# A residual-add RMSNorm whose engines get programs, semaphores and a hardware loop of their own

## The chip, the cores and the metric

The kernel runs on one core of one Trainium2 chip. The metric is device time in microseconds (us), the median of several executions. A profile holds one execution, so a single profile differs from the median by a microsecond or two.

Engines in the profile: DVE is the vector engine, ACT the scalar engine, POOL is GpSimd, SP issues the DMA transfers, and "SPq" is SP's queue. 16 DMA engines move the data; a transfer is dealt out to all of them in packets: chained by their times, the packet records of the kernel before give each engine 1710 to 1714 of the 27392 packets of 57344 bytes, and 16 packets are under way at once for 98% of the time (100 to 3600 us). Tiles are counted from 0, as in the code.

## The reference

```python
batch, seq, dim = 32, 2048, 2048          # all float32
z = x + residual
rms = np.sqrt(np.mean(z ** 2, axis=-1, keepdims=True) + eps)
return (z / rms * gamma).astype(np.float32)
```

Two arrays of 537 MB are read and one is written: 1610.6 MB in all. There is little arithmetic to each byte.

## The kernel before

The 65536 rows are cut into 74 tiles of 128 partitions: 3 rows per partition in the first, 5 in the second, 7 in the other 72. Two slots `z` hold x and are overwritten with the sum and then the result; the residual goes to an area of 11 rows in which two tiles overlap. A tile framework orders the instructions, places the semaphores and writes the loop over tiles out in full.

```python
    def load_r(i):
        a = entry(i)
        nc.sync.dma_start(out=r_area[:, a : a + sizes[i], :], in_=rows(r_f, i))

    def add(i, a, b):
        z = z_slots[i % 2][:, a:b, :]
        o = entry(i)
        nc.vector.tensor_add(out=z, in0=z, in1=r_area[:, o + a : o + b, :])
    # ... square(): ACT, one row at a time, then the root; scale(): DVE ...

    def compute(i):
        # ... (last tile: four parts, interleaved) ...
        done = []
        for a, b in parts(i):                 # two parts
            add(i, a, b)
            done.append((a, b, square(i, a, b)))
        for d in done:
            scale(i, *d)

    # ... first loads, gamma ...
    compute(0)
    for i in range(1, n_tiles):
        store(i - 1)
        compute(i)
        if i + 1 < n_tiles:
            load_r(i + 1)                     # may start when the first add of tile i is through
            load_x(i + 1)                     # may start when store(i - 1) has landed
    store(last)
```

All three large transfers of a tile (7.3 MB each) go through SP's one queue, in the order store, residual, x.

## Time and profile before

The median was 3726.57 us (3726.44 to 3728.58, three runs).

| What | Value | Where it stands |
|---|---|---|
| span of the profiled run | 3724.8 us | head of the page |
| busy: data queue, DVE, ACT | 99.9%, 62%, 29% | queue table; busy table |
| rate in nearly every slice | 434 GB/s | the slices |
| one tile (three transfers of 7.3 MB) | 50.76 us | store to store in SP's timeline |
| instruction fetches | 20 packets of 8 KB | queue table, q14 |

The page of the kernel before: the head, the rate in 40 slices of the span, the DMA queues (packets, MB, share of the 16 engines' time) and the chain that ended last.

```profile
span 3724.8 us, 2571 instructions
DVE 2302.8 (62%) x816; ACT 1072.3 (29%) x1176; POOL 0.2 (0%) x4
GB/s 419 432 434 434 434 434 434 435 434 434 434 434 434 434 434 434 434 434 434 434 432 434 434 434 434 433 434 434 434 434 434 434 434 434 433 434 434 434 435 397
q1 hardware_dynamic: 32832, 1610.63, 99.9%
q14 instruction: 20, 0.16, 0.0%
DMA 67%; DVE 24%; ACT 8%; issue 0%; SPq 0%; DVEq 0%
```

The data queue is busy for 99.9% of the span and moves 434 GB/s in nearly every slice. The chain gives a third of the span to DVE and ACT, but it follows one slot around, and about half of the transfers' time in it is standing in the queue (34.6 us from a store's issue to its landing, 16.9 us of it moving data). An engine share in a chain is therefore not yet a limit.

SP's issues in the timeline of the kernel before (start us, duration us, queue, line, operation, what it moves):

```profile
1994.57 0.34 SPq L92 DMA_DIRECT2D out_dram<-z  x1
2018.89 0.33 SPq L84 DMA_DIRECT2D r_area<-in_residual_dram  x1
2029.14 0.33 SPq L88 DMA_DIRECT2D z<-in_x_dram  x1
2045.33 0.34 SPq L92 DMA_DIRECT2D out_dram<-z  x1
...
2096.09 0.34 SPq L92 DMA_DIRECT2D out_dram<-z  x1
...
2147.41 0.34 SPq L92 DMA_DIRECT2D out_dram<-z  x1
...
2198.17 0.34 SPq L92 DMA_DIRECT2D out_dram<-z  x1
```

From store to store a tile takes 50.76 us (2045.33 less 1994.57, and so on), which is 22.0 MB at 434 GB/s. One step is 51.32 us, from 2096.09 to 2147.41. The residual load is issued at 2018.89, the x load at 2029.14, when the store before has landed.

### The profile page before, as it was taken

The page shows a single profiled execution, that of the slowest core. Times are in us where ns is not written, and L with a number is a line of the kernel's source. Part 1 is how long each engine was busy: PE and PEld are TensorE (multiplying, and loading weights), DVE is VectorE, ACT ScalarE, POOL GpSimd, SP SyncE. Part 2 cuts the span into 40 slices and gives each one's busy share as a digit, 9 for nine tenths or more (in the row PEclk, how much of TensorE's full clock was granted, in tenths as well). Part 3 has the DMA queues.
Part 4 walks back from the last instruction along what each step waited for, and adds up shares of the span by engine and source line. Part 5 has one row for each costly group of instructions (what it writes and reads, how often), then busy time and mean ns, then how long its engine had stood idle before and what let it go on. Part 6 is the DMA issues. An engine that isn't in the chain of part 4 may idle for free.

```text
span 3724.8 us, 2571 instructions
## 1 busy us (share of the span) xinstructions
DVE 2302.8 (62%) x816; ACT 1072.3 (29%) x1176; POOL 0.2 (0%) x4
## 2 busy tenths in 40 slices
DVE  5666665566665566665566665566665566655566
ACT  2333322233322233322233322233322233322233
POOL 0000000000000000000000000000000000000000
DMA  9999999999999999999999999999999999999999
GB/s 419 432 434 434 434 434 434 435 434 434 434 434 434 434 434 434 434 434 434 434 432 434 434 434 434 433 434 434 434 434 434 434 434 434 433 434 434 434 435 397
DMA packets 32860, 1610.82 MB, mean 432 GB/s; under 512 B 3652, under 2 KB 3652, under 8 KB 3652
## 3 DMA queue, kind: packets, MB, share of 16 engines
q1 hardware_dynamic: 32832, 1610.63, 99.9%
q14 instruction: 20, 0.16, 0.0%
q10 hardware_dynamic: 8, 0.03, 0.0%
HBM read 1073.77 MB, written 536.87 MB: 432 GB/s over the span
## 4 chain that ended last, share of the span: by engine, by line
DMA 67%; DVE 24%; ACT 8%; issue 0%; SPq 0%; DVEq 0%
DMA z<-in_x_dram 34%; DMA out_dram<-z 33%; DVE z L97 15%; DVE z L125 9%; ACT sq_junk L103 8%; ACT rms L110 0%; DVE rstd L122 0%; SPq L84 0%; DVEq L97 0%; SPq L88 0%; DVE rstd_tail L122 0%; DVEq L122 0%
## 5 line engine op out<-in xcount | busy, mean ns | idle before, releaser
L97 DVE TENSOR_TENSOR z<-z,r_area 128x8192 f32<-128x8192 f32 (+2 forms) x150 | 1109.4, 7437 | 1272.7 <-DMA z<-in_x_dram 1270.5
L103 ACT ACTIVATE sq_junk<-z 128x2048 f32<-128x2048 f32 x512 | 963.4, 1882 | 2614.7 <-DVE z L97 2603.3
L125 DVE SCALAR_TENSOR_TENSOR z<-z,rstd,gamma_tile 128x2048 f32<-128x2048 f32 x505 | 1153.5, 2344 | 5.2
L122 DVE RECIPROCAL rstd<-rms 128x4 f32<-128x4 f32 (+2 forms) x146 | 25.3, 173 | 117.1 <-ACT rms L110 117.1
L103 ACT ACTIVATION_READ_ACCUMULATOR sq_junk<-z 128x1 f32 x512 | 95.4, 186 | 0.0
L110 ACT ACTIVATE rms<-ssq,eps_tile 128x4 f32<-128x4 f32 (+2 forms) x150 | 44.5, 297 | 4.8
L125 DVE SCALAR_TENSOR_TENSOR z<-z,rstd_tail,gamma_tile 128x2048 f32<-128x2048 f32 x7 | 16.2, 2344 | 0.1
L161 DVE LOAD_MASK_SELECT gamma_tile<-r_area x1 | 0.0, 14 | 11.4 <-DMA r_area<-in_gamma_dram 11.4
L103 ACT ACT_TABLE_LOAD x1 | 1.3, 1283 | 11.1 <-DMA z<-in_x_dram 11.1
L161 DVE STREAM_SHUFFLE gamma_tile<-r_area 128x2048 f32<-128x2048 f32 x1 | 2.3, 2294 | 0.0
L156 DVE MEMSET r_area<- 128x2048 f32 x1 | 1.8, 1765 | 0.4 <-issue 0.4
L110 ACT ACT_TABLE_LOAD x1 | 1.3, 1283 | 0.0
L122 DVE RECIPROCAL rstd_tail<-rms 128x2 f32<-128x2 f32 (+1 forms) x4 | 0.6, 162 | 0.2
L67 DVE MEMSET eps_tile<- 128x1 f32 x1 | 0.1, 59 | 0.8 <-PEq L192 0.8
L192 POOL MEMSET const-bfloat16-1.0<- 128x1 bf16 x1 | 0.1, 101 | 0.0
L192 POOL MEMSET const-uint8-127<- 128x1 uint8 x1 | 0.1, 101 | 0.0
L192 POOL MEMSET const-float32-0.0<- 128x1 f32 x1 | 0.1, 98 | 0.2 <-issue 0.2
L192 POOL MEMSET const-float32-1.0<- 128x1 f32 x1 | 0.1, 98 | 0.0
## 6 DMA issues: line engine op xcount, KB each, us to landing
r_area<-in_residual_dram SPq DMA_DIRECT2D x72, 7168.0 KB, 27.2
z<-in_x_dram SPq DMA_DIRECT2D x71, 7168.0 KB, 33.8
out_dram<-z SPq DMA_DIRECT2D x71, 7168.0 KB, 34.6
z<-in_x_dram SPq DMA_DIRECT2D x3, 2048.0 KB, 24.1
out_dram<-z SPq DMA_DIRECT2D x3, 2048.0 KB, 16.7
r_area<-in_residual_dram SPq DMA_DIRECT2D x1, 5120.0 KB, 29.4
z<-in_x_dram SPq DMA_DIRECT2D x1, 5120.0 KB, 42.5
out_dram<-z SPq DMA_DIRECT2D x1, 5120.0 KB
```

Of the source, the lines that this page charges most:

```text
L67: nc.vector.memset(eps_tile, float(eps))
L97: nc.vector.tensor_add(out=z, in0=z, in1=r_area[:, o + a : o + b, :])
L103: nc.scalar.activation(out=sq_junk, in_=z_slots[i % 2][:, a + g, :], func=Act.Square, accum_out=ssq[:, g : g + 1],)
L110: nc.scalar.activation(out=rms[:, :n], in_=ssq[:, :n], func=Act.Sqrt, bias=eps_tile, scale=inv_d)
L122: nc.vector.reciprocal(out=rstd[:, :n], in_=rms[:, :n])
L125: nc.vector.scalar_tensor_tensor(out=row, in0=row, scalar=rstd[:, g : g + 1], in1=gamma_tile, op0=mult, op1=mult,)
L156: nc.vector.memset(stage, 0.0)
L161: nc.vector.stream_shuffle(gamma_tile, stage, [0] * 32)
L192: nc = _bacc.Bacc("TRN2", target_bir_lowering=False, num_devices=1)
```

## The change

The intent is to take the ordering out of the framework's hands: each engine gets its own program, waits on semaphores named by the kernel, and runs tiles 3 to 70 in a hardware loop of its own, two tiles per iteration (34 iterations). Transfers, their sizes and order, and the vector and scalar instructions stay. The core of the diff, cut:

```diff
-    slots = ctx.enter_context(tc.tile_pool(name="slots", bufs=1))
+    z = [sb(f"z{p}", [P, R, D]) for p in range(2)]
+    names = ["x_in", "r_in", "s_out", "add_a", "add_b", "rms_a", "rms_b", "done"]
+    ev = {k: [sem(f"{k}{p}") for p in range(2)] for k in names}
+    def sp_turn(sp, t):
+        i = t.i
+        t.wait(sp, "done", -1)
+        inc(sp.dma_start(out=t.dram(o_f, o_full, -1), in_=z[(i - 1) % 2][...]), "s_out", i - 1)
+        ...
+        t.wait(sp, "add_a")
+        load_r(sp, t, 1)
+        t.wait(sp, "s_out", -1)
+        ...
+        load_x(sp, t, 1)
+    def dve_turn(v, t, own):
+        t.wait(v, "x_in")
+        t.wait(v, "r_in")
+        (a0, b0), (a1, b1) = parts(i)
+        inc(add(v, i, a0, b0), "add_a", i)
+        inc(add(v, i, a1, b1), "add_b", i)
+        for h, (a, b) in enumerate(parts(i)):
+            t.wait(v, "rms_a" if h == 0 else "rms_b")
+            ...                               # reciprocal, scale
+        inc(ins, "done", i)
+    @block.sync
+    def _(sp):
+        ...                                   # first loads, tiles 1 and 2
+        with sp.Fori(0, 2 * n_iter, 2) as it:
+            for i in range(LO, LO + 2):
+                sp_turn(sp, Turn(i, it))      # wait values and addresses from a register
+        ...                                   # last tiles, written out
+    @block.vector                             # and @block.scalar: the same shape
+    ...
+    nc.gpsimd.sem_clear(range(ids[0], ids[-1] + 1))
-    for i in range(1, n_tiles):
-        store(i - 1)
-        compute(i)
-        ...
```

More of the change, by code (lines that the diff above doesn't have):

```diff
@@ L38 @@
     STEP = 4
-    n_full = n_rows // (P * R)
-    left = (n_rows - n_full * P * R) // P
-    assert n_full * P * R + left * P == n_rows
+    U = 16
     lead = [3, 5]
-    assert left + R == sum(lead)
-    sizes = lead + [R] * (n_full - 1)
+    n_full = (n_rows // P - sum(lead)) // R
+    sizes = lead + [R] * n_full
     starts = [0]
@@ L47 @@
         starts.append(starts[-1] + P * k)
+    assert starts[-1] == n_rows
     n_tiles = len(sizes)
     last = n_tiles - 1
-    assert n_tiles >= 5
+    LO = 3
+    n_iter = (last - 1 - LO) // 2
+    HI = LO + 2 * n_iter
+    assert n_iter >= 1
     def rows(t, i):
@@ L54, in rows, with full, sb, ps @@
         return t[starts[i] : starts[i] + P * k, :].rearrange("(p r) m -> p r m", r=k)
+    def full(t):
+        return t[starts[2] :, :].rearrange("(n p r) m -> n p r m", p=P, r=R)
+    x_full, r_full, o_full = full(x_f), full(r_f), full(o_f)
     inv_d = 1.0 / float(D)
-    slots = ctx.enter_context(tc.tile_pool(name="slots", bufs=1))
-    stats = ctx.enter_context(tc.tile_pool(name="stats", bufs=6))
-    psum = ctx.enter_context(tc.tile_pool(name="psum", bufs=1, space=bass.MemoryType.PSUM))
-    z_slots = [slots.tile([P, R, D], fp32, name=f"z{k}") for k in range(2)]
-    r_area = slots.tile([P, R + STEP, D], fp32, name="r_area")
-    eps_tile = slots.tile([P, 1], fp32, name="eps_tile")
-    sq_junk = psum.tile([P, D], fp32, name="sq_junk")
-    gamma_tile = psum.tile([P, D], fp32, name="gamma_tile")
-    nc.vector.memset(eps_tile, float(eps))
+    def sb(name, shape):
+        return ctx.enter_context(nc.sbuf_tensor(name, shape, fp32))
+    def ps(name, shape):
+        return ctx.enter_context(nc.psum_tensor(name, shape, fp32))
+    sems = []
+    def sem(name):
+        sems.append(ctx.enter_context(nc.semaphore(name)))
+        return sems[-1]
+    ctx.enter_context(tc.tile_critical())
+    z = [sb(f"z{p}", [P, R, D]) for p in range(2)]
+    r_area = sb("r_area", [P, R + STEP, D])
+    eps_tile = sb("eps_tile", [P, 1])
+    ssq = [[sb(f"ssq{p}{h}", [P, 4]) for h in range(2)] for p in range(2)]
+    rms = [[sb(f"rms{p}{h}", [P, 4]) for h in range(2)] for p in range(2)]
+    rstd = [[sb(f"rstd{p}{h}", [P, 4]) for h in range(2)] for p in range(2)]
+    tail_ssq = sb("tail_ssq", [P, R])
+    tail_rms = sb("tail_rms", [P, R])
+    tail_rstd = sb("tail_rstd", [P, R])
+    sq_junk = ps("sq_junk", [P, D])
+    gamma_tile = ps("gamma_tile", [P, D])
+    names = ["x_in", "r_in", "s_out", "add_a", "add_b", "rms_a", "rms_b", "done"]
+    ev = {k: [sem(f"{k}{p}") for p in range(2)] for k in names}
+    x_tail = [sem(f"x_tail{k}") for k in range(4)]
+    g_in = sem("g_in")
+    dve = sem("dve_own")
+    act = sem("act_own")
+    s_tail = sem("s_tail")
+    tail_ev = {k: sem(f"tail_{k}") for k in ("add", "rms", "done")}
+    tail = [(0, 2), (2, 4), (4, 6), (6, 7)]
     def entry(i):
@@ L72, in entry @@
         return 0 if i % 2 else STEP
-    tail = [(0, 2), (2, 4), (4, 6), (6, 7)]
     def parts(i):
@@ L79, in parts @@
             return [(0, 2), (2, sizes[0])]
-        return [(STEP, sizes[i]), (0, STEP)] if i % 2 else [(0, R - STEP), (R - STEP, R)]
-    def load_r(i):
-        a = entry(i)
-        nc.sync.dma_start(out=r_area[:, a : a + sizes[i], :], in_=rows(r_f, i))
-    def load_x(i):
-        for a, b in tail if i == last else [(0, sizes[i])]:
-            nc.sync.dma_start(out=z_slots[i % 2][:, a:b, :], in_=rows(x_f, i)[:, a:b, :])
-    def store(i):
-        for a, b in tail if i == last else [(0, sizes[i])]:
-            nc.sync.dma_start(out=rows(o_f, i)[:, a:b, :], in_=z_slots[i % 2][:, a:b, :])
@@ L94, in add @@
-    def add(i, a, b):
-        z = z_slots[i % 2][:, a:b, :]
-        o = entry(i)
-        nc.vector.tensor_add(out=z, in0=z, in1=r_area[:, o + a : o + b, :])
-    def square(i, a, b):
-        n = b - a
-        ssq = stats.tile([P, 4], fp32, name="ssq")
-        for g in range(n):
-            nc.scalar.activation(
-                out=sq_junk,
-                in_=z_slots[i % 2][:, a + g, :],
-                func=Act.Square,
-                accum_out=ssq[:, g : g + 1],
-            )
-        rms = stats.tile([P, 4], fp32, name="rms")
-        nc.scalar.activation(
-            out=rms[:, :n], in_=ssq[:, :n], func=Act.Sqrt, bias=eps_tile, scale=inv_d
-        )
-        return rms
@@ L115, in scale @@
-    def scale(i, a, b, rms):
-        n = b - a
-        if i == last:
-            rstd = stats.tile([P, 4], fp32, name="rstd_tail", bufs=1)
-        else:
-            rstd = stats.tile([P, 4], fp32, name="rstd")
-        nc.vector.reciprocal(out=rstd[:, :n], in_=rms[:, :n])
-        for g in range(n):
-            row = z_slots[i % 2][:, a + g, :]
-            nc.vector.scalar_tensor_tensor(
-                out=row,
-                in0=row,
-                scalar=rstd[:, g : g + 1],
-                in1=gamma_tile,
+        k = sizes[i] if i < 2 else R
@@ new lines, in parts, with __init__, at, wait @@
+        return [(STEP, k), (0, STEP)] if i % 2 else [(0, R - STEP), (R - STEP, R)]
+    class Turn:
+        def __init__(self, i, it=None):
+            self.i, self.it, self.p = i, it, i % 2
+        def at(self, d):
+            n = ((self.i + d) // 2 + 1) * U
+            return n if self.it is None else self.it * (U // 2) + n
+        def wait(self, eng, kind, d=0):
+            eng.wait_ge(ev[kind][(self.i + d) % 2], self.at(d))
+        def dram(self, t, t_full, d):
+            if self.it is None:
+                return rows(t, self.i + d)
+            return t_full[self.it + (self.i + d - 2)]
@@ new lines, in inc, with load_x, load_r @@
+    def inc(ins, kind, i):
+        return ins.then_inc(ev[kind][i % 2], U)
+    def load_x(sp, t, d=0):
+        i = t.i + d
+        inc(sp.dma_start(out=z[i % 2][:, : sizes[i], :], in_=t.dram(x_f, x_full, d)), "x_in", i)
+    def load_r(sp, t, d=0):
+        i = t.i + d
+        e = entry(i)
+        inc(
+            sp.dma_start(out=r_area[:, e : e + sizes[i], :], in_=t.dram(r_f, r_full, d)),
+            "r_in",
+            i,
+        )
+    def sp_turn(sp, t):
+        i = t.i
+        t.wait(sp, "done", -1)
+        inc(
+            sp.dma_start(out=t.dram(o_f, o_full, -1), in_=z[(i - 1) % 2][:, : sizes[i - 1], :]),
+            "s_out",
+            i - 1,
+        )
+        if t.it is None and i == last:
+            return
+        t.wait(sp, "add_a")
+        load_r(sp, t, 1)
+        t.wait(sp, "s_out", -1)
+        if t.it is None and i + 1 == last:
+            for k, (a, b) in enumerate(tail):
+                sp.dma_start(
+                    out=z[last % 2][:, a:b, :], in_=rows(x_f, last)[:, a:b, :]
+                ).then_inc(x_tail[k], U)
+        else:
+            load_x(sp, t, 1)
@@ L130, in scale, with add @@
+    def add(v, i, a, b):
+        e = entry(i)
+        s = z[i % 2][:, a:b, :]
+        return v.tensor_add(out=s, in0=s, in1=r_area[:, e + a : e + b, :])
+    def scale(v, i, a, b, rs, c=0):
+        for g in range(a, b):
+            s = z[i % 2][:, g, :]
+            ins = v.scalar_tensor_tensor(
+                out=s,
+                in0=s,
+                scalar=rs[:, c + g - a : c + g - a + 1],
+                in1=gamma_tile[:, :],
                 op0=mult,
@@ L132, in scale @@
             )
-    def compute(i):
-        if i == last:
-            before = None
-            for a, b in tail:
-                add(i, a, b)
-                rms = square(i, a, b)
-                if before is not None:
-                    scale(i, *before)
-                before = (a, b, rms)
-            scale(i, *before)
-            return
-        done = []
-        for a, b in parts(i):
-            add(i, a, b)
-            done.append((a, b, square(i, a, b)))
-        for d in done:
-            scale(i, *d)
@@ L153, in load_gamma @@
-    def load_gamma():
-        row = R
-        stage = r_area[:, row, :]
-        nc.vector.memset(stage, 0.0)
-        for q in range(4):
-            nc.scalar.dma_start(
-                out=r_area[32 * q : 32 * q + 1, row, :], in_=gamma.partition_broadcast(1)
-            )
-        nc.vector.stream_shuffle(gamma_tile, stage, [0] * 32)
-    load_x(0)
-    load_r(0)
-    load_gamma()
-    load_r(1)
-    load_x(1)
-    compute(0)
-    for i in range(1, n_tiles):
-        store(i - 1)
-        compute(i)
-        if i + 1 < n_tiles:
-            load_r(i + 1)
-            load_x(i + 1)
@@ L175 @@
-    store(last)
+        return ins
+    def dve_turn(v, t, own):
+        i, p = t.i, t.p
+        t.wait(v, "x_in")
[4 more added lines that the diff above has]
+        for h, (a, b) in enumerate(parts(i)):
+            n = b - a
+            t.wait(v, "rms_a" if h == 0 else "rms_b")
+            v.reciprocal(out=rstd[p][h][:, :n], in_=rms[p][h][:, :n]).then_inc(dve, U)
+            v.wait_ge(dve, own(i, h))
+            ins = scale(v, i, a, b, rstd[p][h])
+        inc(ins, "done", i)
@@ new lines, with __init__, wait, next @@
+    class Chain:
+        def __init__(self, eng, s):
+            self.eng, self.s, self.n, self.base = eng, s, 0, None
+        def wait(self):
+            if self.n:
+                self.eng.wait_ge(self.s, self.n if self.base is None else self.base + self.n)
+        def next(self, ins):
+            ins.then_inc(self.s, 1)
+            self.n += 1
+    def act_part(s, chain, src, a, b, sq, rm):
+        for g in range(a, b):
+            if g > a:
+                chain.wait()
+            chain.next(
+                s.activation(
+                    out=sq_junk[:, :],
+                    in_=src[:, g, :],
+                    func=Act.Square,
+                    accum_out=sq[:, g - a : g - a + 1],
+                )
+            )
+        chain.wait()
+        return s.activation(
+            out=rm, in_=sq[:, : b - a], func=Act.Sqrt, bias=eps_tile[:, :], scale=inv_d
+        )
@@ new lines, in act_turn @@
+    def act_turn(s, t, chain):
+        i, p = t.i, t.p
+        for h, (a, b) in enumerate(parts(i)):
+            chain.wait()
+            t.wait(s, "add_a" if h == 0 else "add_b")
+            inc(
+                act_part(s, chain, z[p], a, b, ssq[p][h], rms[p][h][:, : b - a]),
+                "rms_a" if h == 0 else "rms_b",
+                i,
+            )
+    block_ctx = nc.Block()
+    block = block_ctx.__enter__()
+    @block.sync
+    def _(sp):
+        load_x(sp, Turn(0))
+        load_r(sp, Turn(0))
+        load_r(sp, Turn(1))
+        load_x(sp, Turn(1))
+        for i in range(1, LO):
+            sp_turn(sp, Turn(i))
+        with sp.Fori(0, 2 * n_iter, 2) as it:
+            for i in range(LO, LO + 2):
+                sp_turn(sp, Turn(i, it))
+        for i in range(HI, n_tiles):
+            sp_turn(sp, Turn(i))
+        for k, (a, b) in enumerate(tail):
+            sp.wait_ge(tail_ev["done"], k + 1)
+            sp.dma_start(
+                out=rows(o_f, last)[:, a:b, :], in_=z[last % 2][:, a:b, :]
+            ).then_inc(s_tail, U)
+        sp.wait_ge(s_tail, U * len(tail))
+        sp.wait_ge(ev["s_out"][(last - 1) % 2], ((last - 1) // 2 + 1) * U)
@@ new lines, in _, with tail_scale @@
+    @block.vector
+    def _(v):
+        row = R
+        v.memset(eps_tile[:, :], float(eps))
+        v.memset(r_area[:, row, :], 0.0).then_inc(tail_ev["add"], 1)
+        v.wait_ge(g_in, 4 * U)
+        v.stream_shuffle(gamma_tile[:, :], r_area[:, row, :], [0] * 32)
+        for i in range(LO):
+            dve_turn(v, Turn(i), lambda i, h: (2 * i + h + 1) * U)
+        with v.Fori(0, 2 * n_iter, 2) as it:
+            for i in range(LO, LO + 2):
+                dve_turn(v, Turn(i, it), lambda i, h: it * (2 * U) + (2 * i + h + 1) * U)
+        for i in range(HI, last):
+            dve_turn(v, Turn(i), lambda i, h: (2 * i + h + 1) * U)
+        base = 2 * last * U
+        t = Turn(last)
+        t.wait(v, "r_in")
+        def tail_scale(k):
+            a, b = tail[k]
+            v.wait_ge(tail_ev["rms"], k + 1)
+            v.reciprocal(out=tail_rstd[:, a:b], in_=tail_rms[:, a:b]).then_inc(dve, U)
+            v.wait_ge(dve, base + (k + 1) * U)
+            scale(v, last, a, b, tail_rstd, a).then_inc(tail_ev["done"], 1)
+        for k, (a, b) in enumerate(tail):
+            v.wait_ge(x_tail[k], U)
+            add(v, last, a, b).then_inc(tail_ev["add"], 1)
+            if k:
+                tail_scale(k - 1)
+        tail_scale(len(tail) - 1)
@@ new lines, in _ @@
+    @block.scalar
+    def _(s):
+        s.wait_ge(tail_ev["add"], 1)
+        for q in range(4):
+            s.dma_start(
+                out=r_area[32 * q : 32 * q + 1, R, :], in_=gamma.partition_broadcast(1)
+            ).then_inc(g_in, U)
+        chain = Chain(s, act)
+        for i in range(LO):
+            act_turn(s, Turn(i), chain)
+        with s.Fori(0, 2 * n_iter, 2) as it:
+            n = chain.n
+            chain.base = it * R
+            for i in range(LO, LO + 2):
+                act_turn(s, Turn(i, it), chain)
+            assert chain.n - n == 2 * R
+        chain.base = None
+        chain.n = n + 2 * R * n_iter
+        for i in range(HI, last):
+            act_turn(s, Turn(i), chain)
+        for k, (a, b) in enumerate(tail):
+            chain.wait()
+            s.wait_ge(tail_ev["add"], k + 2)
+            act_part(
+                s, chain, z[last % 2], a, b, tail_ssq[:, a:b], tail_rms[:, a:b]
+            ).then_inc(tail_ev["rms"], 1)
@@ L179 @@
+    block_ctx.__exit__(None, None, None)
+    ids = [a.num for a in sems]
+    assert ids == list(range(ids[0], ids[0] + len(ids)))
+    nc.gpsimd.sem_clear(range(ids[0], ids[-1] + 1))
 _INS = ['x', 'residual', 'gamma', 'eps']
```

## The prediction

> **What bounds the kernel now.** Data movement. The page's DMA queue table has the one data queue busy for 99.9% of 16 engines' span, and the rate by slice is 434 GB/s in nearly every slice. [...] 1610.6 MB at 434 GB/s is 3711 us; the span is 3724.8. DVE is 62% busy, ACT 29%. The chain of waits looks like a loop through one slot (x load 33.8 us, compute 33.0, store 34.6 per two tiles), but half of each load and store there is standing in the queue behind another 7.3 MB transfer (16.9 us each), so compute is not the limit.
>
> **Slack, read from the timeline around 1910-2000 us.** A store is issued when a whole x load is still ahead of it (17 us to spare). The residual load is issued 6.6 us after x landed, with the previous store still having 10.2 us to go. The x load is issued with a whole residual load ahead. So the sequencers may lose about 10 us in each tile before the DMA queue runs dry.
>
> **What the change does.** The same transfers, sizes, addresses, order on the one SP queue, the same DVE and ACT instructions with the same waits (ACT waited on its own semaphore between squares before too). Added per tile: register arithmetic, waits against registers, a compare and branch per two tiles, DMA issues with register addresses (0.34 us now; I expect under 1 us). All is well under 2 us per tile against 10 us of slack: worth 0. Added once: block entry branches, a closing barrier and the semaphore clear, about +1 to +3 us in all. In the tail, chunk 1 is now scaled ahead of chunk 3's add; DMA stays busy there, so worth 0 to -1 us.
>
> **Instruction fetch.** The page has 20 packets, 0.16 MB, on the instruction queue: 8 KB each, which the trace shows as 0.31 us on one DMA engine. As a transfer ends with its slowest of 16 engines, some fetches stretch a tile: most tiles take 50.76 us from store to store, a few just after a fetch 51.1 to 51.3. I estimate -2 to -4 us [...]. [...]
>
> **Predicted:** 3726 us, 8 in 10 between 3719 and 3742. Faster by over 2%: 0.01; within 2%: 0.97; slower by over 2%: 0.02.
>
> **What would show each step right.** DMA still at 434 GB/s in all middle slices; store-to-store still 50.76 us per tile; the SP queue's waits on DVE and on stores about as long as before; the instruction queue's packets fall to about 6 to 10. Wrong: slices under 430 GB/s at regular intervals of 101.5 us (loop branches drain the queue), hundreds of instruction packets (loop refetches), DVE idle before its add longer than 18 us, or SP issue times over 5 us.
>
> **What would make it wrong.** A loop branch that stalls SP by more than 10 us each iteration; register-addressed DMA issues that [...] split transfers differently (packets other than 57 KB); a costly exit.

The sum: the terms that stand (0 per tile, +1 to +3 us once, 0 to -1 us in the tail, -2 to -4 us by fewer fetches) come to -4 to +1 us on a median of 3726.57, and the forecast is 3726 us. The condition of the -2 to -4 us is cut; it was that the loops fetch no instructions once they run, and the page of the changed kernel has 2 packets on the instruction queue.

## The result, and the profile after

The changed kernel took 3726.74 us (median of 4, 3726.27 to 3729.7) beside 3726.81 us of the kernel before (4 runs). The ratio is 1.0001 with a 95% interval of 0.9983 to 1.0018. Ratios here are the mean time of one kernel's fast runs over that of the other's of the same rounds, so not quite the ratio of the medians.

The page of the changed kernel, the same lines:

```profile
span 3724.2 us, 4147 instructions
DVE 2302.6 (62%) x816; ACT 1072.4 (29%) x1176; POOL 0.2 (0%) x4
GB/s 420 430 434 434 434 434 434 434 434 434 434 434 434 434 434 434 433 434 434 434 434 434 434 434 434 435 434 434 435 434 434 434 435 434 434 434 434 434 434 400
q1 hardware_dynamic: 32832, 1610.63, 100.0%
q14 instruction: 2, 0.02, 0.0%
DMA 66%; DVE 22%; issue 9%; ACT 2%; SPq 0%; DVEq 0%; ACTq 0%
```

The instruction queue fell from 20 packets to 2. The rate did not move: 434 GB/s in nearly every slice, as before. The profile records 4147 instructions where there were 2571. The busy instructions are the same (x816 on DVE, and ACT and POOL likewise), so the 1576 more are register arithmetic, waits and branches. They appear nowhere in the time. SP's issues in the timeline of the changed kernel, at the same place:

```profile
1995.61 0.36 SPq L158 DMA_DIRECT2D out_dram<-z  x1
2019.75 0.33 SPq L149 DMA_DIRECT2D r_area<-in_residual_dram  x1
2029.86 0.33 SPq L143 DMA_DIRECT2D z<-in_x_dram  x1
2046.38 0.36 SPq L158 DMA_DIRECT2D out_dram<-z  x1
...
2097.12 0.36 SPq L158 DMA_DIRECT2D out_dram<-z  x1
...
2147.89 0.36 SPq L158 DMA_DIRECT2D out_dram<-z  x1
...
2198.66 0.35 SPq L158 DMA_DIRECT2D out_dram<-z  x1
```

The steps shown are now 50.74 to 50.77 us; the 51.32 is gone. A store is issued 0.18 us after its last scaling (0.03 before; from DVE's timeline, not shown) and in 0.36 us (0.34 before). That is what register addresses and register waits cost a tile: the changed kernel with its loops written out (below) has 0.03 and 0.34 again.

Two profiles of each kernel, cut into stages (the second pair comes from the experiments; the second profile before is of a single run). First packet and last landing are read from the packet records of the trace, the rest from SP's timeline. "Tile 4" is the fifth tile; the expectations further down call its store, at 216.5 us in the kernel before, "tile 3's", and so are off by one.

| Stage, us | before | before again | after | after again |
|---|---|---|---|---|
| start to first packet | 1.74 | 1.74 | 1.96 | 1.97 |
| first packet to store of tile 4 | 214.8 | 215.6 | 217.0 | 217.0 |
| store of tile 4 to store of tile 72 | 3455.8 | 3456.8 | 3452.0 | 3453.4 |
| store of tile 72 to last landing | 51.3 | 51.3 | 51.3 | 51.3 |
| last landing to end | 1.2 | 1.2 | 1.9 | 1.9 |
| span | 3724.8 | 3726.6 | 3724.2 | 3725.6 |

So the null result is a sum. By the means of each pair the middle gains 3.6 us, the start and the exit lose 0.9, and the first tiles, up to the store of tile 4, lose 1.8. These terms rest on two profiles each; runs of one kernel differ by up to 4 us, so the medians alone can't tell them apart. In the kernel before, 10 and 9 of the 68 middle steps are over 50.9 us; above 50.76 these add up to 4.9 and 5.4 us. In the changed kernel there are none in either profile. That covers the gain; it is less than their sum, as some short steps follow long ones before (50.41 after 51.19), and as late steps of the changed kernel are some hundredths longer (see the last section).

Each long step holds an instruction fetch or comes right after a step that holds one; the reverse doesn't hold, and about half of the fetches have no long step by them. From the packet records of the kernel before (four of the 20; times from the trace's own zero, 11.0 us ahead of the span's start): an 8 KB packet of the instruction queue takes 0.31 us, and the data packet that starts as it ends, so by the times on the same engine, takes 2.36 to 2.60 us, where 2.12 is usual. The last three have a long step by them, the first has none.

```
fetch starts   takes     57344-byte packet starts   takes
554.85         0.309     555.16                     2.360
1874.95        0.316     1875.25                    2.598
2077.80        0.309     2078.10                    2.365
2484.44        0.309     2484.74                    2.362
```

A fetch costs the engine that carries it about 0.55 us or more (0.31 plus 0.25 to 0.48), and all 16 engines must finish a transfer: in the changed kernel the first engine is through with a store at 2024.89 us and the last at 2029.38, and the x load that waits for this store is issued at 2029.86. What shows in the time is less where that engine isn't the last one: 3.6 us for the 18 fetches that fell away are 0.2 us each.

### The profile page after: what moved, and what is told of

The parts are those of the page before. It is cut to its first block, busy times and chain, and to the rows that moved or that the text cites. A ratio compares the mean times of both kernels' runs of the same rounds, so it can differ in the third digit from the quotient of the medians.

```text
span 3724.2 us, 4147 instructions
## 1 busy us (share of the span) xinstructions
DVE 2302.6 (62%) x816; ACT 1072.4 (29%) x1176; POOL 0.2 (0%) x4
## 3 DMA queue, kind: packets, MB, share of 16 engines
HBM read 1073.77 MB, written 536.87 MB: 432 GB/s over the span
## 4 chain that ended last, share of the span: by engine, by line
DMA 66%; DVE 22%; issue 9%; ACT 2%; SPq 0%; DVEq 0%; ACTq 0%
DMA out_dram<-z 33%; DMA z<-in_x_dram 33%; DVE z L179 15%; DVE z L184 7%; ACT sq_junk L230 1%; DMA r_area<-in_residual_dram 0%; ACT rms L238 0%; DVE rstd L204 0%; SPq L158 0%; DVEq L130 0%; ACTq L218 0%; ACTq L130 0%; DVE tail_rstd L298 0%; SPq L143 0%; SPq L169 0%
## 5 line engine op out<-in xcount | busy, mean ns | idle before, releaser
L184 DVE SCALAR_TENSOR_TENSOR z<-z,tail_rstd,gamma_tile 128x2048 f32<-128x2048 f32 x7 | 16.2, 2345 | 0.1
```

The costliest lines, as they stand in the source:

```text
L184: ins = v.scalar_tensor_tensor(out=s, in0=s, scalar=rs[:, c + g - a : c + g - a + 1], in1=gamma_tile[:, :], op0=mult, op1=mult,)
```

## The experiments

All twelve gave right results. Four theories were at stake: that the fetches make the 3.6 us; that the loops cost something which the fetches hide; that the compute chain bounds the kernel and not the queue; and that about 10 us of each tile are to spare.

### Both kernels again, and the loops written out

`rep_after` and `rep_before` are the two kernels unaltered. `unrolled` is the changed kernel without its loops:

```diff
-        with sp.Fori(0, 2 * n_iter, 2) as it:
-            for i in range(LO, LO + 2):
-                sp_turn(sp, Turn(i, it))
+        for i in range(LO, HI):
+            sp_turn(sp, Turn(i))
     # and the same for DVE and ACT
```

> The changed kernel, unaltered, a second time. Theory (the data queue bounds both kernels, and the change only shifts a few microseconds: about -3.8 us in the middle from removed instruction fetches, about +0.2 at the start, +0.7 at the exit, +2.2 in the first four tiles): the same time as before within 0.1%; instruction queue again at 2 packets; the tile step again 50.75 to 50.79 us in every middle tile. If the +2.2 us of the first four tiles is the kernel's own doing it comes again (the store of tile 3 is issued at about 219 us against 216.5 before); if it is chance it moves by a microsecond or more. Rival (a loop has a cost of its own that chance hid): slower by 0.2% or more here.

> The kernel before, unaltered, for a second profile. Theory: 20 packets on the instruction queue again, and again about six tiles of 51.1 to 51.3 us among steps of 50.76. The issue of tile 3's store tells how much the first four tiles vary by chance: 216.5 us in the first profile; a difference of more than 1 us says that the early 2.4 us between the two kernels need no cause in the change.

> The changed kernel with its hardware loops written out, so that only the explicit semaphores, the separate programs and the closing block are left of the change. Theory (the loop's whole effect is that it fetches no instructions): the instruction packets come back, 15 to 20 of them, each with one data packet beside it that is late; some tile steps of 51.1 to 51.3 us come back; the span is 2 to 4 us longer than that of the changed kernel with loops, so 0 to +0.15% against before. Rival 1 (the loops cost time that the saved fetches pay for): the span gets shorter than with loops. Rival 2 (the steadier middle comes from the explicit semaphores, not from the loop): steps stay at 50.75 to 50.79 without loops.

Measured beside 9 runs of the kernel before with a median of 3726.39 us: `rep_after` 3726.96 us (5 runs, ratio 1.0000, 0.9987 to 1.0014), `unrolled` 3729.32 us (5 runs, 3729.13 to 3730.53, ratio 1.0007, 0.9994 to 1.0021), `rep_before` 3728.4 us (one run). The instruction queue of `unrolled`:

```profile
q14 instruction: 22, 0.18, 0.0%
```

With the loops written out the fetches come back, 22 of them, and with them ten long steps (6.6 us together above 50.76). The two kernels differ by the loops alone (with the registers that they need), and their runs, taken side by side, don't overlap: the fastest `unrolled` run, 3729.13, lies above the slowest `rep_after` run, 3727.70. (Of the four earlier runs of the changed kernel one took 3729.70, and three of the nine of the kernel before here took 3728.5 to 3729.1; five against five is what the figure rests on.) The loops are worth 2.4 us by the medians. So the loops gain, the programs and the closing block lose about as much, and both rivals fall: the loops don't cost, and explicit semaphores alone don't make the middle steady. One expectation of `rep_after` failed: its steps are 50.76 only up to about tile 51 and 50.81 to 50.86 from there to the end, but for one of 50.67. Why is not known (see the last section).

### Instruction fetches by themselves

`pool_pages` gives the idle GpSimd a program that touches nothing the kernel uses. It needs 512 instructions in each of 34 iterations:

```diff
+    @block.gpsimd
+    def _(g):
+        with g.Fori(0, 34, 1) as _it:
+            for k in range(512):
+                g.memset(filler[:, k : k + 1], 0.0)
+            g.drain()
```

`act_pages` lengthens ACT's loop body from some 55 instructions (counted in the program) to some 185, at its end, where ACT is idle:

```diff
                 act_turn(s, Turn(i, it), chain)
+            for k in range(128):
+                s.mul(filler[:, k + 1 : k + 2], filler[:, 0:1], 0.0)
+            s.drain()
```

> The changed kernel with a program on GpSimd, otherwise idle: a loop of 34 iterations over 512 one-column fills, about 0.1 us each. It touches nothing that the kernel uses, so it adds instruction fetches alone: 512 instructions are four pages, about 136 packets in the first half of the run. Theory (a fetch takes about 0.55 us of the DMA engine that carries it, always the same one for an engine's program): up to 136 times 0.55, +75 us, if nothing else limits; if the fetches are spread over the 16 DMA engines, about a sixteenth, +5 us. Rival (the steadier middle of the changed kernel has nothing to do with fetches): no change.

> The changed kernel with 128 tiny activations (one element per partition) and a drain at the end of ACT's loop body, where ACT is idle for 33 us in each tile. The body of about 60 instructions grows to about 190, more than one 8 KB fetch of 128 instructions. Theory (a loop that doesn't fit fetches again in each iteration, and a fetch costs the one DMA engine that carries it about 0.55 us, which shows in full when that engine is the slowest): one to three packets in each of the 34 iterations, 35 to 100 in all, and +10 to +50 us. [...] Rival (fetches are free): 35 to 100 packets and no change in time.

Measured: `pool_pages` 3874.75 us (5 runs, ratio 1.0396, 1.0382 to 1.0411), `act_pages` 3726.95 us (5 runs, ratio 1.0001, 0.9988 to 1.0015). The page of `pool_pages`: busy tenths of POOL in 40 slices, the rate in the same slices, and the instruction queue.

```profile
POOL 5655655555200000000000000000000000000000
GB/s 397 393 353 390 370 353 391 370 362 384 383 418 422 424 433 434 434 432 435 435 434 432 434 434 435 433 434 434 434 434 434 434 434 434 435 433 434 434 435 395
q14 instruction: 204, 1.67, 0.1%
```

The slices in which POOL runs are the slow ones; when POOL is through the rate is at 418 to 424 for three slices, and then back at 434. 202 packets more than in the changed kernel cost 148 us (the difference of its mean time to that of the kernel before), or 0.73 us each. The prediction of the fetch's price holds in kind and was low in number: more packets came than I expected (6 per iteration, not 4) and each cost 0.73, not 0.55. The records name no engine, but on a busy engine each packet starts within a few ns of the end of the one ahead. Chained by these times, 196 of 203 fetches lie on the same chain as the fetch before them. That chain spends 68 us on the fetches, and its data packets take 81 us more than at 2.116 us each: 149 us, the whole loss. On the 15 others data packets take 32 us more on average (1.8 in the changed kernel over the same stretch). So up to 32 of the 81 us may have another cause, of which the fills on GpSimd, writing to SBUF, are a rival not tested by itself.

The timeline of POOL in `pool_pages` (xN merges N instructions; in brackets the idle time before them):

```profile
400.46 2.37 POOL L342 MEMSET filler<- 128x1 f32 x70 [0.50 <-issue]
410.03 1.97 POOL L342 MEMSET filler<- 128x1 f32 x58 [7.20 <-issue]
414.86 4.28 POOL L342 MEMSET filler<- 128x1 f32 x128 [2.85 <-issue]
419.74 4.28 POOL L342 MEMSET filler<- 128x1 f32 x128 [0.61 <-issue]
426.75 4.28 POOL L342 MEMSET filler<- 128x1 f32 x128 [2.73 <-issue]
431.67 2.37 POOL L342 MEMSET filler<- 128x1 f32 x70 [0.64 <-issue]
```

Blocks of 128 instructions (64 bytes each by estimate, if a block is one packet of 8 KB), with a wait at nearly every border: 0.5 to 2.9 us within the body, and 7.20 us at 410.03. The loop starts over there (58, three times 128 and 70 make up the 512; the 7.20 us hold the drain and the branch too). Over all 33 restarts it is 5.5 to 8.8 us, with a median of 7.2. This loop, with 6 packets in each iteration, thus stalls its engine for some 7 us per iteration, while the data moves at 373 GB/s (mean from 300 to 900 us; 433 in the changed kernel).

The instruction queue of `act_pages`:

```profile
q14 instruction: 3, 0.02, 0.0%
```

A body of some 185 instructions fetched nothing in the loop. The theory's condition, that more than 128 instructions would be fetched again, is refuted. Some 185 instructions on ACT were not fetched again and about 515 on GpSimd were; where between them this turns, and whether the two engines are alike in it, no run here shows. The loops of the changed kernel are shorter than both: its trace records 57 instructions on ACT, 36 on DVE and 20 on SP in one iteration (1995.5 to 2097.0 us).

### How much of a tile is to spare

`late2`, `late4`, `late6`, `late8` and `late15` delay everything that an x tile's arrival sets off, by an idle operation on DVE over 1, 2, 3, 4 or 7 rows (here `late8`). They have 5, 4, 4, 4 and 2 runs:

```diff
         (a0, b0), (a1, b1) = parts(i)
+        if t.it is not None:
+            for a, b in ((0, 4),):            # late15: ((0, 4), (4, 7))
+                same = z[p][:, a:b, :]
+                v.tensor_max(out=same, in0=same, in1=same)
+            v.drain()
         inc(add(v, i, a0, b0), "add_a", i)
```

> The changed kernel with an idle operation (the maximum of four rows with themselves, in place, about 8.6 us by the duration of the addition of as many rows) ahead of the first addition in each of the 68 tiles in the loop. It delays everything that a tile's arrival sets off: residual load, squares, scaling, store. Theory (10.2 us of slack, read from the issue of the residual load to the end of the store before it): no change, under 5 us in all. Rival (the chain of waits, in which a third of the time is compute, is the bound): half of 8.6 us in each tile, about +290 us (+8%).

> As the run before it, but with all seven rows, about 15.2 us, so beyond the slack. Theory: 15.2 less 10.2 us of slack leaves 5 us in each of 68 tiles in which the data queue stands empty: a tile step of about 55.7 us, about +340 us (+9%). Rival (compute chain): half of 15.2 in each tile, +517 us. If slack is really 17 us, as for the store, no change.

These two gave neither the expected threshold at 10.2 us nor half of the delay.

(Rate in 40 slices and data queue on the page of `late8`.)

```profile
GB/s 416 409 412 414 413 405 414 414 414 414 405 414 414 414 415 413 413 405 420 410 413 413 414 413 415 414 414 407 412 414 414 414 414 414 414 413 406 413 422 415
q1 hardware_dynamic: 32832, 1610.63, 98.7%
```

(The same on the page of `late15`.)

```profile
GB/s 418 359 391 364 366 365 364 392 365 366 365 362 377 374 373 365 364 366 391 364 366 365 360 388 373 366 365 365 366 391 364 366 365 361 395 365 365 357 399 416
q1 hardware_dynamic: 32832, 1610.63, 89.0%
```

`late8` took 3901.53 us (ratio 1.0467, 1.0451 to 1.0483; its tiles take 53.3 us), `late15` 4321.84 us (1.1596, 1.1575 to 1.1617; 59.5 us a tile). I formed a second theory, a threshold at 6.5 us, and tried shorter delays:

> The idle operation of the first delay runs with two rows, about 4.4 us by the duration of an addition of as many. The 8.7 us and 15.2 us delays gave tile steps of about 53.3 and 59.4 us, both 44.2 us plus the delay, not 40.4 plus the delay as predicted. Mended theory (a threshold at 50.76 less 44.2, about 6.5 us): a step of 50.76 still, no change, under 5 us in all. Rival (half of the delay is paid in each tile): 68 times 2.2, +150 us (+4%).

> The same with three rows, about 6.6 us. Mended theory: just at the threshold, a step of 50.76 to 51.1 us, 0 to +25 us in all. Rival (half): +223 us (+6%).

`late4` took 3778.45 us (1.0133, 1.0117 to 1.0149) and `late6` 3871.63 us (1.0384, 1.0363 to 1.0404). The second theory fell too: 4.4 us cost 52 us where it had nothing to cost, and 6.6 us cost 145. Half of the delay (150 and 223) is not paid either. The packet records of the five tell where the time goes. For 55 middle tiles of each kernel I added up by how much the 57344-byte packets exceed 2.116 us, per DMA engine and tile (the excess), and took the median time between the first and the last of the 16 engines to finish a transfer (the spread).

```
kernel      delay us   mean step us   packets' excess us   empty queue   spread of engines us
before      0          50.81          0.04                 -             4.8
after       0          50.76          0.04                 -             4.5
act_pages   0          50.79          0.05                 -             3.2
late2       2.29       50.77          0.04                 -             3.7
late4       4.42       51.51          0.74                 -             3.5
late6       6.56       52.80          1.74                 0.6%          2.5
late8       8.69       53.33          1.90                 1.3%          0.8
late15      15.24      59.51          1.85                 11.0%         0.6
```

The empty share is 100% less the share of the data queue on each page, where that is below 99.9%. The excess pays for all of what `late4` loses (0.74 of 0.75 us in each tile) and most of what `late6` does (1.74 of 2.04; 0.6% of 52.8 us of empty queue, 0.3 us, is the rest). `late8` adds 1.3% of 53.3 us, 0.7 us, of empty queue, and together with 1.90 that is its whole loss of 2.57. `late15` has 6.5 us of empty queue. The slow packets stand at two places: where the x load gives way to the store, and where the store gives way to the residual load. In `late8` they start 6 to 9 us after the issue of the store and 27 to 30 us after it. The idle operation itself runs from 11 to 20 us after that issue, and in those bins the excess is 0.00: what costs comes with the lateness, and not while the operation reads and writes SBUF.

SP's issues in `late8`:

```profile
1938.09 0.35 SPq L158 DMA_DIRECT2D out_dram<-z  x1
1964.70 0.33 SPq L149 DMA_DIRECT2D r_area<-in_residual_dram  x1
1966.11 0.33 SPq L143 DMA_DIRECT2D z<-in_x_dram  x1
1991.33 0.36 SPq L158 DMA_DIRECT2D out_dram<-z  x1
```

Here the x load follows the residual load at 1.4 us, where it followed at 10 us in the changed kernel. The residual load comes when the store ahead of it is nearly over.

My reading before the last run was this. The 16 engines run some 4.5 us apart, and so they don't all turn from reading to writing at the same moment. The lead of the fast ones lasts only while the next transfer is queued before they are through. By the traces, a store takes 16.4 us from DVE's start on the x tile, a residual load is issued 6.7 us plus the delay after it, and its first packet starts 1.0 us later. That leaves 8.7 us less the delay for the spread: 4.3, 2.1 and 0 for `late4`, `late6` and `late8`, against 3.5, 2.5 and 0.8 measured. For 2.3 us it leaves 6.4, which is more than the spread needs.

> The idle operation with one row, about 2.3 us. In the traces of the longer delays the added time lies in data packets that run slow at the turns between loads and stores (0.7 us per engine and tile at a delay of 4.4, 1.7 at 6.6, 1.9 at 8.7) and, from 8.7 on, in an empty queue; and the spread between the first and the last of the 16 engines to finish a transfer falls from about 4.5 us to 3.5, 2.5 and 0.8. Theory (the spread keeps the engines from turning together; it can last only while the residual load is issued before the first engine is through with the store: 16.4 less 6.7 less the delay less 1.0 to the first packet, so 8.7 less the delay): at 2.3 us the spread may be 6.4, more than the 4.5 that the engines have anyway, so no change, under 10 us in all. Rival (each microsecond of delay costs, in proportion as the 4.4 us delay did): about half of 52, +27 us (+0.7%).

`late2` took 3726.94 us (5 runs, ratio 1.0003, 0.9989 to 1.0017), where the proportional rival had +27 us. So 2.3 us are free and 4.4 are not. That a smaller spread makes the packets slow, though, the traces speak against. `act_pages` has a smaller spread than `late4` (3.2 beside 3.5) and no slow packets. Within `late4`, the quarter of the tiles with the smallest spread after the x load (3.0 us) has an excess of 0.38, and the quarter with the largest (4.0 us) has 1.05. What does go with the slow packets where the store gives way to the residual load is how long before the first engine is through with the store this load is issued: 5.2 us in the changed kernel and 3.6 in `late2` (excess there 0.00), 1.8 in `late4` (0.17), 0.6 in `late6` (0.70) and 0.1 in `late8` (0.74). Where the x load gives way to the store the excess is larger (0.56, 1.02 and 1.14), though the store has been queued for 9.8 us when the first engine gets to it (10.8 in `late2`, where the excess is 0.00). Its cause is open.

### The slower first tiles

`gamma16` splits each load of gamma over 16 engines; `lo5` starts the loops two tiles later.

```diff
-                out=r_area[32 * q : 32 * q + 1, R, :], in_=gamma.partition_broadcast(1)
+                out=r_area[32 * q : 32 * q + 1, R, :].rearrange("p (k m) -> p k m", k=16),
+                in_=gamma.partition_broadcast(1).rearrange("p (k m) -> p k m", k=16),
```

```diff
-    LO = 3
+    LO = 5
```

> The changed kernel with each of the four loads of gamma split in 16 pieces of 512 bytes, so that 16 DMA engines share it, where one engine now carries 4 packets of 0.31 us. Theory (all bytes are dealt equally to 16 engines and the slowest one sets the end): if the engine that carries gamma is the slowest one, up to 1.2 us less; if it isn't, no change. Either way within 0.05% of the changed kernel.

> The changed kernel with the hardware loops starting at tile 5 and not at tile 3 (33 iterations, 5 tiles written out ahead of them). Four profiles with loops issue tile 3's store at 218.3 to 219.0 us, three without at 216.5 to 217.3. If entering the loop costs this, tile 3's store comes at about 217.1 us here, as in the kernel written out, and the lag shows two tiles later; if the lag has another source, it is at 218.3 to 219.0 us here too. Total time: within 0.05% of the changed kernel either way.

`gamma16` took 3727.13 us (ratio 1.0000, 0.9987 to 1.0014), `lo5` 3726.8 us (1.0001, 0.9987 to 1.0014). Tile 4's store ("tile 3's" in the expectations) was issued at 218.57 us and 218.76 us, so late in both. In `lo5` that store is the first that SP's loop issues, but the lag is there before: tile 2's store, written out in `lo5`, comes at 120.88 us, beside 120.60 in the changed kernel and 119.23 in the kernel before. So neither gamma's engine nor entering the loop is the cause. The kernel written out had tile 4's at 217.09. Five profiles with loops (with this place otherwise as in the changed kernel) have 218.3 to 219.0 us, three without have 216.5 to 217.3. The source of these 1.8 us stays open.

No version tried beats either kernel. At 434 GB/s there is little left to win: 1610.6 MB at that rate take 3711 us of the 3725, and no slice of a page shown here is above 435.

## Why the prediction was right or wrong, point by point

- **The time.** 3726 us predicted, 3726.74 us measured, inside the range; "within 2%" was given 0.97. Right. That it came to within a microsecond is in part luck: 1.8 us that nobody foresaw (last point) stand against what the foreseen terms gain.
- **What bounds the kernel.** Right: the data queue. The share of DVE and ACT in the chain is no limit: a 2.3 us delay in each of 68 tiles, 156 us of work in all, cost nothing.
- **Added per tile: worth 0.** Right. 1576 more recorded instructions changed nothing; SP's issue of a store is later by 0.15 us and longer by 0.02 us at most.
- **Added once: +1 to +3 us.** Measured +0.9 (0.2 at the start, 0.7 at the exit), just under the range. Neither was taken apart further.
- **The tail: 0 to -1 us.** 0.0: from the store of tile 72 to the last landing it is 51.3 us in both.
- **Instruction fetch: -2 to -4 us.** Right: -3.6 us in the middle, and 2.4 us between the loops and the loops written out. The 2 packets left are fewer than the 6 to 10 expected.
- **The opposite case, loops that fetch again in each iteration.** It didn't occur. In `pool_pages`, where one DMA engine carries nearly all the fetches (196 of 203), a packet cost 0.73 us (the scattered fetches of the kernel before cost 0.2), and a loop that was fetched again stalled its engine for about 7.2 us at each restart, longer than the slack really is. What it costs if SP's or DVE's loop is fetched again was not run.
- **"About 10 us in each tile".** Wrong: between 2.3 and 4.4 us. The failing step was to read the slack from one transfer's end to the next one's issue, as if the 16 engines were one. The fast engines are through some 4.5 us earlier, so the residual load is issued 5.2 us ahead of the first of them and not 10.2; its first packet comes 1.0 us after the issue, and packets get slower before any queue is empty (0.74 us a tile in `late4`). The verdict survived because the change adds about 0.2 us to a tile.
- **Not foreseen:** the tiles up to the store of tile 4, +1.8 us, cause open.

## What to carry to other kernels

When one shared resource is busy for 99.9% of the span, at a rate that no slice of a page shown exceeds by more than 1 GB/s (434 here), price a change first by what it takes from or gives to that resource: here, neither 1576 more instructions nor a new way of ordering mattered, but 18 instruction fetches of 8 KB did, at about 0.2 us each, and 202 on one DMA engine did at 0.73 us each. Test slack by spending it in small doses; the distance between two events in a timeline (10.2 us) was an upper bound here (between 2.3 and 4.4 us were to spare), because 16 engines, some 4.5 us apart, stand behind each event and not one. The hardware loops cost nothing here, and saved the fetches (2 packets with them, 22 with the loops written out); check that in the count of packets on the instruction queue.

## What the traces showed that the prediction did not have

- Instruction fetches beside a busy data queue cost time: each 8 KB packet cost the run 0.73 us in `pool_pages`, and GpSimd waited 0.5 to 2.9 us at most borders in the stretch shown.
- The restart of a loop that is fetched again took about 7.2 us in `pool_pages`, drain included.
- One core held 434 GB/s for reads and writes together (HBM read 1073.77 MB and written 536.87 MB, by the page of the kernel before).
- Packets at the turns between load and store got slower when the next work came late, though the queue wasn't empty: 2.12 us each without a delay, and in `late4`, with the data queue busy for 99.9% of the span, an excess of 0.74 us per engine and tile. The cause is open.
- The 16 engines drift apart under a steady load. In each of the six profiles with loops and neither further fetches nor a costly delay, the tile step goes from 50.76 to about 50.83 us at some tile and stays there but for a step or two: from 726 us on in `gamma16` (58 steps, 4 us in all, as much as the fetches it saved), later in `act_pages`, `rep_after`, `late2` and `lo5`, and in the last six steps of the first profile after the change. From then on the spread grows by about the same amount with each tile (in `gamma16` from 3.8 us at tile 10 to 7.3 at tile 58): an engine falls behind, and it shows once it is the last. In the first profile after the change the second to last engine falls behind from about tile 43 (2.7 us after the first engine at tile 40, 4.5 at tile 64), before the steps get longer. Why it falls behind is open.
